# Value heads 1 to 3 as one job of seven half-size products

## The chip, the cores and the metric

The kernel runs on one core of a Trainium2 chip. The metric is the device time of one execution in microseconds, lower is better. The core has five engines with an instruction stream each: TensorE (PE, matmuls, with weight loads in PEld), VectorE (DVE), ScalarE (ACT), GpSimd (POOL) and SyncE (SP), which issues the DMAs. SBUF holds the working tiles, PSUM the matmuls' results, HBM everything that is stored between stages.

## The reference

One layer of a hybrid decoder, T = 1024 tokens, width D = 1024. A normalised input h is projected by one matrix w_in into all that follows. Four heads of gated linear attention (GLA) take a query and key of 128, a value of 256, a rank-16 decay code and a gate each; eight heads of stick-breaking attention take 128 each; two merge gates weigh the branches.

```python
h = rmsnorm(x, norm_g)
qg, kg, vg, gg, r, qs, ks, vs, gs, m = split(h @ w_in)   # vg: 1024 columns = 4 heads of 256
log_a = log_sigmoid(r @ w_dec_up + b_dec) / 16
y_a = (rmsnorm(gla(qg, kg, vg, log_a), gla_g) * silu(gg)) @ w_pa
y_b = (stick_breaking(qs, ks, vs) * silu(gs)) @ w_pb
out = rmsnorm(x + (sigmoid(ma) * y_a + sigmoid(mb) * y_b) @ w_o, final_g)
```

Everything is float32. The change touches vg = h @ w_in[:, value columns], the way in which it is stored, and sums of blocks of h.

## The kernel before

Precision comes from splitting: each float32 operand is written as a high part that TensorE takes in one pass (the copy on ACT rounds it) and a low part, the rest (a subtraction on DVE). A product then is three matmuls, high by high, high by low, low by high. The helper `split` makes the two parts.

**First stage** (pool p0). For each of the eight blocks of 128 tokens: `norm_a` squares and sums x on ACT, `norm_b` scales it on DVE, `turn_x` transposes it on PE into a PSUM tile `tr`, one for each half g of the columns, and splits the result into the quarter blocks `hq[n, g]` (n: first or second 512 tokens). These are named ha11, ha12, ha21, ha22, with h or l for the parts. In the gaps `first_v` computes value head 0 and the decay code, 272 columns, for the block before.

**Value stage.** `v_unit` makes heads 1 to 3 in 24 units (three heads, eight blocks), each 24 matmuls of 256 columns in `proj_n` (L221). Each result is split by ACT and DVE into a staged tile `o` and stored in its two parts in `d_gv` by `store_v`, two blocks a DMA. Beside it POOL puts the blocks together again (`whole`, high + low), and forms the sums S1 to S4 of quarter blocks (`sum2`); ACT and DVE split them (`part`). A list `line` sets which of these stands beside which unit.

**Pairs.** From there every projection is a job of seven products of half size, after Winograd: with the block sums S1 to S4 of h, and sums T1 to T4 of the weights, seven products of 512 x 512 x 512 take the place of eight. The class `Pairs` runs the jobs one after another: the 1 MB load of a job's weights (tile `raw`), the sums of its weights on POOL (`tt`), four splits, seven units. Its first two loads and first three splits are issued when `Pairs` is made. Beside job 0 the decay code is made from the rank-16 result: `wup` is loaded, `wst` and `rst` are split from it and from the turned `rcode`, and a matmul of the two gives the decay's logits. The first unit's product is copied out by ACT (`f`), and the third unit needs that copy done, since it goes on in the same PSUM bank.

**Later.** The GLA stage loads values and gates a block at a time (`gl_load`) and works on it in `gl_local`; then stick-breaking attention and output.

SP issues all DMAs in its program's order. ACT, DVE and PE take their instructions in program order as well; in the value stage of before the order of ACT and DVE is that of the code (`manual_schedule`), elsewhere a planner sets it.

Of the kernel before, what the change touches and what calls it, by code (L numbers as in the profile page):

```python
# [67 lines left out]
class Pairs:  # L68
# [33 lines left out]
def hybrid_layer(ctx: ExitStack, tc: tile.TileContext, x, norm_g, w_in, w_up, b_dec,  # L102
# [20 lines left out]
    def dram_set(nm, count, shape, dt=F32):  # L123
        return [dram.tile(shape, dt, tag=f"{nm}{i}", name=f"d_{nm}{i}") for i in range(count)]
# [220 lines left out]

    vend = const.tile([P, SB_H, NT], F32, tag="vend", name="vend")

    def store_v(key, i, tb):

        if tb % 2:  # L350
            nc.sync.dma_start(d_gv[i][:, tb - 1:tb + 1], vst.pop((key, tb // 2)).bitcast(F32))

    def v_stage(key, tb):
        if tb % 2 == 0:
            vst[key, tb // 2] = (stage().rearrange("p a b -> p (a b)")
                                 .rearrange("p (t s c) -> p t s c", t=2, s=2))
        return vst[key, tb // 2][:, tb % 2]

    with tc.tile_pool(name="p0", bufs=3, reuse_waits="tile") as p0:
        gb = p0.tile([P, D], F32, tag="gb", name="gb", bufs=1)  # L360
# [40 lines left out]
        ws0.append(load_vr(1))  # L401
        for tb in range(2, NT):
            load_x(tb)

        def first_v(tb):
            pt = proj_n(rows_of(ws0), hq, tb, VR, early=tb == 0)
            st = v_stage(0, tb)
            split(pt[:, 0:DV], st[:, 0], st[:, 1])
            store_v(0, 0, tb)
            nc.vector.tensor_copy(rcode[:, tb], pt[:, DV:VR])  # L410

        def turn_x(tb, gs=(0, 1)):
            xs = by_parity(xss[tb])
            for g in gs:
                pt = ps.tile([P, HALF], F32, tag="tr", name="tr")
                for j in range(4):
                    nc.tensor.transpose(pt[:, j * P:(j + 1) * P], xs[:, g, j], ident)
                cs = slice(tb % 4 * P, (tb % 4 + 1) * P)
                q = hq[tb // 4, g]
                split(pt.rearrange("p (a b) -> p a b", a=4), q[0][:, :, cs], q[1][:, :, cs])  # L420

        with tc.manual_schedule(engines={mybir.EngineType.Activation, mybir.EngineType.DVE}):
            norm_a(0)
# [15 lines left out]
            norm_a(1)  # L439
            nc.vector.tensor_sub(lo0, raw0, hi0.bitcast(F32))  # L440
            nc.scalar.activation(hi1, raw1, AF.Copy)
            norm_b(1, 0)
            nc.vector.tensor_sub(lo1, raw1, hi1.bitcast(F32))
            norm_b(1, 1)
            ws0 = [w[1:] for w in ws0]
            for tb in range(1, NT):
                if tb + 1 < NT:
                    norm_a(tb + 1)
                turn_x(tb)
                if tb + 1 < NT:  # L450
                    norm_b(tb + 1)
                first_v(tb - 1)
            first_v(NT - 1)
        load_cols(p0.tile([22, P], F32, tag="vrow", name="vrow", bufs=1))


    v_ctx = ExitStack()
    vw = v_ctx.enter_context(tc.tile_pool(name="vw", bufs=2, reuse_waits="tile"))
    vws, vraw = {}, {}

    def v_load(c0, key):
        vraw[key] = raw_tile()
        nc.sync.dma_start(vraw[key], w_in[:, c0:c0 + DV].rearrange("(k p) c -> p k c", p=P))

    def v_split(key, i):

        hi, lo = ((vw.tile([P, 4, DV], F32R, tag="v" + s, name="v" + s) if i else
                   w_tile(s).rearrange("p k c -> p (k c)").rearrange("p (k c) -> p k c", c=DV)) for s in "hl")
        split(vraw[key][:, 4 * i:4 * i + 4], hi, lo)
        vws.setdefault(key, []).append((hi, lo))  # L470
# [10 lines left out]
    vjobs = [(i, C_GV + i * DV) for i in range(1, GLA_H)]  # L481
    v_load(vjobs[0][1], vjobs[0][0])
    v_load(vjobs[1][1], vjobs[1][0])
    vline = []
    for i, (key, _) in enumerate(vjobs):
        for tb in range(NT):
            vline.append((lambda key=key, tb=tb: v_unit(key, tb), True))
            if tb in (3, 4) and i + 1 < len(vjobs):
                vline.append((lambda key=vjobs[i + 1][0], a=tb - 3: v_split(key, a), False))
            if tb == 5 and i + 2 < len(vjobs):  # L490
                vline.append((lambda job=vjobs[i + 2]: v_load(job[1], job[0]), False))
    st = Line(vline)


    f = {}

    def fresh(nm):
        f[nm] = ev.tile([P, HALF], F32, tag="f", name="f")
        return f[nm]

    def whole(nm, q, j):
        return lambda: nc.gpsimd.tensor_add(fresh(nm), q[0][:, j].bitcast(F32), q[1][:, j].bitcast(F32))

    def sum2(nm, a, b, op=ALU.subtract):
        return lambda: nc.gpsimd.tensor_tensor(fresh(nm), f[a], f[b], op=op)

    def part(nm, j):
        def go():
            if nm not in comb:
                comb[nm] = quarter(a21b, nm, "a21") if nm == "S2" else quarter(sp, nm, nm.lower())  # L510
            split(f[nm], comb[nm][0][:, j], comb[nm][1][:, j])

        return go

    line = [[] for _ in range(25)]
    for j in range(4):
        ops = [whole("a21", hq[1, 0], j), whole("a22", hq[1, 1], j), sum2("S1", "a21", "a22", ALU.add),
               whole("a11", hq[0, 0], j), sum2("S3", "a11", "a21"), sum2("S2", "S1", "a11"),
               whole("a12", hq[0, 1], j), sum2("S4", "a12", "S2")]
        at = [(8 * j + i) * 22 // 32 for i in range(8)]  # L520
        for i, op in enumerate(ops):
            line[at[i]].append(op)
        for i, nm in ((2, "S1"), (4, "S3"), (5, "S2"), (7, "S4")):
            line[at[i] + 2].insert(0, part(nm, j))

    manual = ExitStack()
    manual.enter_context(tc.manual_schedule(engines={mybir.EngineType.Activation, mybir.EngineType.DVE}))
    for a in range(2):
        v_split(vjobs[0][0], a)
    st.run(1)  # L530
    for i, s in enumerate("hl"):
        nc.sync.dma_start(d_a21[i], hq[1, 0][i].bitcast(F32))
    for ops in line:
        for op in ops:
            op()
        st.run(1)
    manual.close()


    def qk_pair(c0, i, dst):  # L540
        def evict(J, n, bank, add):
# [97 lines left out]
    st.run()  # L639
    v_ctx.close()  # L640
    a21_ctx.close()
    late = []
    pairs = Pairs([merge_pair(C_MA, i, d_ga) for i in range(3)] +
                  gla_qk(0) + [gg_pair(0), gg_pair(1)] + gla_qk(1) + [gg_pair(2), gg_pair(3)] +
                  [f for i in range(4) for f in (qk_pair(C_SQ, i, d_q), qk_pair(C_SK, i, d_k))] +
                  [sg_pair(i) for i in range(3)] + [merge_pair(C_MB, i, d_gb) for i in range(4)] +
                  [sv_pair(i) for i in range(4)] + [merge_pair(C_MA, 3, d_ga)], late)

    dq_ctx = ExitStack()
    dq = dq_ctx.enter_context(tc.tile_pool(name="dq", bufs=1, reuse_waits="tile"))  # L650
# [844 lines left out]
```

## Time and profile before

| | us |
|---|---|
| median of 3 runs | 1190.33 (1189.4 to 1190.63) |
| profiled execution, span | 1187.3 |
| profiled execution, own device time | not recorded, only its span |
| PE busy | 1174.5 |
| DVE busy | 834.8 |
| ACT busy | 535.3 |
| POOL busy | 294.4 |

Times are from the start of the span. "Busy" is when an engine executes; what a row waits for stands in square brackets behind it, as the idle time before it and the instruction that ended it. Matmuls overlap in PE's pipeline, so that a row's duration is longer than the distance to the next start; the distance between starts is what a matmul costs in a row of many. For a DMA the row of SP is only its issue; the landing is given in a line of its own as the smallest, middle and largest time from issue to landing.

### The profile page before, as it was taken

How to read it: one execution, taken by the hardware profiler on the slowest of the kernel's cores; microseconds unless marked ns; L12 is line 12 of the kernel's file. 1: busy time of each engine (PE TensorE's matmuls, PEld its weight loads, DVE VectorE, ACT ScalarE, POOL GpSimd, SP SyncE). 2: the span in 40 equal slices, each digit the busy share in tenths (PEclk: the TensorE clock that was granted, in tenths of full speed). 3: DMA queues.
4: the chain of work that ended last, by engine and by line, in shares of the span. 5: the costliest groups of instructions: out<-in, count | busy, mean ns of one | idle time of the engine just before them, and what ended most of it. 6: DMA issues, size and time to landing. Idle time of an engine off the chain costs nothing.

```text
span 1187.3 us, 17020 instructions
## 1 busy us (share of the span) xinstructions
PE 1174.5 (99%) x6051; PEld 989.3 (83%) x6051; DVE 834.8 (70%) x1388; ACT 535.3 (45%) x1000; POOL 294.4 (25%) x249
## 2 busy tenths in 40 slices
PE   8999999999999999999999999999999999999997
PEld 8999878888888888888888887888888888888886
DVE  6475876787677777767656567547787876488986
ACT  5343763333444444444434444334444544275543
POOL 1496513143333233224223223000000000700001
PEclk9999999999999999999999999999999999999999
DMA  7434349998356566655454447899766556848652
GB/s 286 196 133 153 129 164 317 331 316 275 120 187 222 183 213 215 188 187 169 145 168 149 133 138 229 254 322 320 258 218 224 186 168 192 288 160 285 220 195 106
DMA packets 189377, 247.65 MB, mean 209 GB/s; under 512 B 12358, under 2 KB 121948, under 8 KB 187756
## 3 DMA queue, kind: packets, MB, share of 16 engines
q1 hardware_dynamic: 188716, 245.52, 61.6%
q8 instruction: 47, 0.77, 0.3%
q10 hardware_dynamic: 576, 1.05, 0.2%
q14 instruction: 38, 0.31, 0.1%
HBM read 154.25 MB, written 92.27 MB: 208 GB/s over the span
## 4 chain that ended last, share of the span: by engine, by line
PE 89%; DVE 4%; ACT 2%; DMA 2%; issue 1%; SPq 0%; POOL 0%; ACTq 0%; DVEq 0%
PE pp L268 15%; PE pp L269 15%; PE pp L270 15%; PE pp L221 8%; PE pp L204 3%; PE pp L203 3%; PE pp L202 3%; PE tr L990 1%; PE av L1013 1%; PE av L1012 1%; PE av L1011 1%; PE z L972 1%; PE z L974 1%; PE z L973 1%; PE xb L1379 1%
## 5 line engine op out<-in xcount | busy, mean ns | idle before, releaser
L164 DVE TENSOR_TENSOR wl<-tt,wh 128x1024 fp32r<-128x1024 f32 x62 | 77.5, 1250 | 53.2 <-ACT wh L163 52.9
L307 DVE TENSOR_TENSOR f<-pp,f 128x512 f32<-128x512 f32 x93 | 64.0, 688 | 72.1 <-PE pp L270 68.2
L242 POOL TENSOR_TENSOR tt<-raw 128x512 f32<-128x512 f32 x31 | 44.6, 1438 | 225.2 <-DVE wl L164 204.8
L163 ACT ACTIVATE wh<-tt 128x1024 fp32r<-128x1024 f32 x62 | 65.6, 1058 | 74.7 <-PE pp L269 68.8
L274 ACT ACTIVATE f<-pp 128x512 f32<-128x512 f32 x93 | 55.1, 593 | 88.2 <-PE pp L270 84.9
L978 DVE TENSOR_TENSOR_SCAN be<-be,m 128x128 f32<-128x128 f32 (+3 forms) x64 | 86.1, 1347 | 4.5 <-ACT be L975 4.3
L163 ACT ACTIVATE wh<-raw 128x1024 fp32r<-128x1024 f32 x44 | 46.5, 1059 | 84.0 <-PE pp L269 48.1
L164 DVE TENSOR_TENSOR wl<-raw,wh 128x1024 fp32r<-128x1024 f32 x44 | 64.3, 1463 | 18.7 <-ACT wh L163 18.1
L229 POOL TENSOR_TENSOR r<-r,nhalf 128x1 f32<-128x1 f32 x40 | 24.4, 609 | 198.3 <-DVE r L228 177.2
L1162 POOL TENSOR_TENSOR N<-A,A 128x512 f32<-128x512 f32 x4 | 6.6, 1658 | 244.0 <-PE pp L204 244.0
L975 ACT ACTIVATE be<-z 128x384 f32<-128x384 f32 (+4 forms) x96 | 47.1, 495 | 19.7 <-PE z L974 17.3
L268 PE MATMUL pp<-ha11h,wh 128*128 128x512 f32 x124 | 49.2, 397 | 0.0
L268 PE MATMUL pp<-S2h,wh 128*128 128x512 f32 x124 | 49.1, 396 | 0.0
L268 PE MATMUL pp<-S1h,wh 128*128 128x512 f32 x124 | 49.1, 396 | 0.0
L268 PE MATMUL pp<-ha12h,wh 128*128 128x512 f32 x124 | 49.0, 395 | 0.0
L268 PE MATMUL pp<-ha22h,wh 128*128 128x512 f32 x124 | 48.9, 394 | 0.2 <-DVE f L307 0.2
L268 PE MATMUL pp<-S3h,wh 128*128 128x512 f32 x124 | 48.8, 394 | 0.0
L268 PE MATMUL pp<-S4h,dh 128*128 128x512 f32 x124 | 48.6, 392 | 0.0
L270 PE MATMUL pp<-S1h,wl 128*128 128x512 f32 x124 | 48.4, 390 | 0.0
L270 PE MATMUL pp<-ha11h,wl 128*128 128x512 f32 x124 | 48.4, 390 | 0.0
L269 PE MATMUL pp<-S2l,wh 128*128 128x512 f32 x124 | 48.3, 390 | 0.0
L270 PE MATMUL pp<-ha12h,wl 128*128 128x512 f32 x124 | 48.3, 390 | 0.0
(519 smaller groups left out, 3844.4 us busy)
## 6 DMA issues: line engine op xcount, KB each, us to landing
raw<-in_w_in_dram SPq DMA_DIRECT2D x34, 1024.0 KB, 6.0
d_gv<-o SPq DMA_DIRECT2D x16, 512.0 KB, 2.6
d_t<-t SPq DMA_DIRECT2D x16, 512.0 KB, 6.4
v<-d_gv SPq DMA_DIRECT2D x32, 256.0 KB, 3.0
d_ogl<-o SPq DMA_DIRECT2D x64, 128.0 KB, 2.6
d_q<-o SPq DMA_DIRECT2D x16, 512.0 KB, 3.8
d_k<-o SPq DMA_DIRECT2D x16, 512.0 KB, 3.5
d_v<-o SPq DMA_DIRECT2D x32, 256.0 KB, 2.5
```

The costliest lines, as they stand in the source:

```text
L163: nc.scalar.activation(hi, src, AF.Copy)
L164: eng.tensor_sub(lo, src, hi.bitcast(F32))
L202: nc.tensor.matmul(pt, whi[:, kb], h_, start=kb == 0, stop=False)
L221: nc.tensor.matmul(pt[:, 0:n], *ops[kb][i], start=k == 0, stop=k == 3 * KB - 1)
L242: nc.gpsimd.tensor_sub(t1, b[:, 0, 1], b[:, 0, 0])
L268: nc.tensor.matmul(pt, bh[:, j], ah[:, j], start=first and j == 0, stop=False, skip_group_check=True)
L269: nc.tensor.matmul(pt, bh[:, j], al[:, j], start=False, stop=False, skip_group_check=True)
L270: nc.tensor.matmul(pt, bl[:, j], ah[:, j], start=False, stop=j == 3, skip_group_check=True)
L274: nc.scalar.activation(t[nm], t[bank], AF.Copy)
L307: nc.vector.tensor_add(add, bank, add)
L975: nc.scalar.activation(om[:, off + pc * w:off + (pc + 1) * w], zt[:, 0:w], AF.Sigmoid, scale=-inv_sqrt)
L978: nc.vector.tensor_tensor_scan(rest, rest, m1[:, off:T][:, ::-1], 1.0, op0=ALU.mult, op1=ALU.max)
```

## The change

The values of heads 1 to 3, 768 columns, become one job of the same seven-product form: halves of 512 tokens by halves of 512 rows by halves of 384 columns. There are 56 items (`v_item`): seven products, two row halves `jp`, four token blocks t, each six matmuls of 384 columns. That makes 336 matmuls instead of 576 of 256 columns.

- **Whole blocks** of h are no longer rebuilt from their parts by POOL. ACT copies each turned block from PSUM in the first stage (`whole`), 16 copies of 128x512.
- **Sums of h** S1 to S4 are made on DVE (`h_sum`), 16 of 128x512, and split (`h_split`); the sums of the value weights T1 to T4 too (`vq_sum`, four of 128x1536). The weights are split in 14 parts of 768 columns (`vq_split`), three of these inside the first stage at blocks 4, 5 and 6.
- **Results** are added up by ACT and DVE (`v_evict`) in tiles s1, s5, p7 and c and stored unsplit by 40 small DMAs (`v_put`, 64 or 128 KB). c has two tiles, "dh" and "dl". `d_gv` holds one value instead of two parts; `gl_local` splits each loaded block (one more split of 128x256 for each of 32 blocks). Head 0's result is copied once instead of split.
- **The order** of PE, ACT and DVE in the job is written out: the table `due` gives the items after which the sums, splits and evictions stand. The two first loads and three first splits of the pair jobs (`pairs.first`) stand at items 40, 46, 49, 53 and 55.
- The x tiles and first weights move to other slots of the same memory; the weight half B22 is loaded after the first stage.

The core of the diff:

```diff
-        for j in self.jobs[:2]:
-            j["load"]()
-        for s in range(3):
-            self.jobs[0]["split"][s]()
+        self.first = [j["load"] for j in self.jobs[:2]] + self.jobs[0]["split"][:3]
...
-    d_gv = dram_set("gv", GLA_H, [P, NT, 2, DV])
+    d_gv = dram_set("gv", GLA_H, [P, NT, DV])
...
+    VPRODUCTS = [("A11", "B11"), ("A12", "B21"), ("A22", "T4"), ("S1", "T1"), ("S2", "T2"), ("S4", "B22"), ("S3", "T3")]
+    def vq_split(u, jp):
+        src = vq[VPRODUCTS[u][1]][:, 2 * jp:2 * jp + 2]
...
+        split(src, hi, lo)
+    def vq_sum(nm):
...
+        nc.vector.tensor_sub(dst, vq[x1], vq[x2_])
+    VW_AT = {4: (0, 0), 5: (0, 1), 6: (1, 0)}
+    def whole(tb, g, pt):
...
+        nc.scalar.activation(wh[n, g, t], pt, AF.Copy)
...
         def first_v(tb):
             pt = proj_n(rows_of(ws0), hq, tb, VR, early=tb == 0)
-            st = v_stage(0, tb)
-            split(pt[:, 0:DV], st[:, 0], st[:, 1])
-            store_v(0, 0, tb)
+            st = v_stage(tb)
+            nc.vector.tensor_copy(st[:, tb % 2], pt[:, 0:DV])
+            if tb % 2:
+                nc.sync.dma_start(d_gv[0][:, tb - 1:tb + 1], st)
...
                 split(pt.rearrange("p (a b) -> p a b", a=4), q[0][:, :, cs], q[1][:, :, cs])
+                whole(tb, g, pt.rearrange("p (a b) -> p a b", a=4))
...
-    def v_unit(i, tb):
-        st = v_stage(i, tb)
-        split(proj_n(rows_of(vws[i]), hq, tb), st[:, 0], st[:, 1])
-        store_v(i, i, tb)
...
-        return lambda: nc.gpsimd.tensor_add(fresh(nm), q[0][:, j].bitcast(F32), q[1][:, j].bitcast(F32))
...
-        return lambda: nc.gpsimd.tensor_tensor(fresh(nm), f[a], f[b], op=op)
...
+    vq_load("B22")
     for i, s in enumerate("hl"):
         nc.sync.dma_start(d_a21[i], hq[1, 0][i].bitcast(F32))
...
+    def v_put(n, J, t, c):
+        tb = 4 * n + t
+        for h, c0, o0, w in (((1, 0, 0, DV), (2, 0, DV, P)) if J == 0 else ((2, P, 0, P), (3, 0, P, DV))):
+            nc.sync.dma_start(d_gv[h][:, tb, c0:c0 + w], c[:, o0:o0 + w])
...
+    def v_item(u, jp, t, bank):
+        (ah, al), (bh, bl) = comb[VPRODUCTS[u][0]], vsp[u, jp]
+        ts = slice(t * P, (t + 1) * P)
+        for i in range(2):
+            j = 2 * jp + i
+            nc.tensor.matmul(bank, ah[:, j, ts], bh[:, i], start=u < 4 and j == 0, stop=False, skip_group_check=True)
...
+        elif u == 5:
+            c = sw.tile([P, 4, P], F32, tag="d" + "hl"[t % 2], name="c", bufs=1).rearrange("p a c -> p (a c)")[:, 0:VH]
+            nc.scalar.activation(c, vy[t], AF.Copy)
+            nc.vector.tensor_add(c, vx[t], c)
+            v_put(0, 1, t, c)
...
+    for u in range(7):
+        if u != 4:
+            for t in range(4):
+                due[8 * u + 5 + t].insert(0, (v_evict, (u, t)))
+    for k, fn in zip((40, 46, 49, 53, 55), pairs.first):
+        at(k, fn)
...
+        t["v"] = split2(t["vr"], [P, DV], "v")
```

In the first stage, ACT between two norms, before (blocks 4 and 5; `o` is head 0's result):

```order
L387 ACTIVATE xs,ssq<-xt 128x1024
L163 ACTIVATE ha21h<-tr 128x4x128
L163 ACTIVATE ha22h<-tr 128x4x128
L163 ACTIVATE o<-pp 128x256
L387 ACTIVATE xs,ssq<-xt 128x1024
```

and now (w, f, o here are the whole blocks):

```order
L433 ACTIVATE xs,ssq<-xt 128x1024
L160 ACTIVATE ha21h<-tr 128x4x128
L403 ACTIVATE w<-tr 128x512
L160 ACTIVATE ha22h<-tr 128x4x128
L403 ACTIVATE o<-tr 128x512
L160 ACTIVATE wh<-vq 128x768
L433 ACTIVATE xs,ssq<-xt 128x1024
```

Each whole copy stands ahead of the next high half, and waits on DVE's low half of the same tile. DVE at block 6, now:

```order
L456 COPY vst<-pp 128x256
L459 COPY rcode<-pp 128x16
L161 TENSOR_TENSOR wl<-vq,wh 128x768
L225 TENSOR_SCALAR r<-ssq 128x1
L381 TENSOR_TENSOR vq<-raw,vq 128x1536
L161 TENSOR_TENSOR ha21l<-tr,ha21h 128x4x128
L161 TENSOR_TENSOR ha22l<-tr,ha22h 128x4x128
```

The sum T1 (128x1536) and a weight split stand ahead of the block's low halves; before, only the small row of `r` stood there. SP in the sixth product, now (c_1144, c_1159 and so on are the tiles c of blocks t = 0, 1, 2, 3; the first and third share a buffer, and the second and fourth):

```order
L655 DMA d_gv2_134<-c_1144 128x128
L655 DMA d_gv3_135<-c_1144 128x256
L235 DMA raw_1164<-in_w_in_dram 128x8x256
L655 DMA d_gv2_134<-c_1159 128x128
L655 DMA d_gv3_135<-c_1159 128x256
L655 DMA d_gv2_134<-c_1177 128x128
L655 DMA d_gv3_135<-c_1177 128x256
```

The 1 MB load of the second pair job stands between the stores of t = 0 and those of t = 1. SP where the value stage ends, before:

```order
L238 DMA raw<-in_w_in_dram 128x8x256
L351 DMA d_gv_134<-o 128x1024
L238 DMA raw<-in_w_in_dram 128x8x256
L351 DMA d_gv_134<-o 128x1024
L351 DMA d_gv_135<-o 128x1024 x3
L655 DMA wup<-in_w_dec_up_dram 16x512
L351 DMA d_gv_135<-o 128x1024
L582 DMA d_ga_142<-f 128x512
```

and now:

```order
L655 DMA d_gv_134<-s_995 128x128
L655 DMA d_gv_135<-s_995 128x256
L655 DMA d_gv_133<-p_912 128x256
L655 DMA d_gv_134<-p_912 128x128
L235 DMA raw<-in_w_in_dram 128x8x256
L744 DMA wup<-in_w_dec_up_dram 16x512
L564 DMA d_ga_142<-f 128x512
```

The load of wup stood ahead of the last value store; it now stands behind all of them and behind the load of the third pair job.

More of the change, by code (lines that the diff above doesn't have):

```diff
@@ new lines, in hybrid_layer, with four @@
+    VW_AT = {4: (0, 0), 5: (0, 1), 6: (1, 0)}
+    wh = {}
+    def four(i, nm):
+        return slot(i, [P, 4 * HALF], nm).rearrange("p (t j c) -> p t j c", t=4, c=P)
+    def whole(tb, g, pt):
+        n, t = divmod(tb, 4)
+        if (n, g) == (0, 1):
+            wh[n, g, t] = ev.tile([P, HALF], F32, tag="f", name="f").rearrange("p (j c) -> p j c", c=P)
+        elif (n, g) == (1, 1):
+            if t % 2 == 0:
+                two = stage().bitcast(F32)
+                for i in range(2):
+                    wh[n, g, t + i] = two[:, i].rearrange("p (j c) -> p j c", c=P)
+        elif t == 0:
+            w = four((3, 5)[n], "w")
+            for i in range(4):
+                wh[n, g, i] = w[:, i]
+        nc.scalar.activation(wh[n, g, t], pt, AF.Copy)
@@ L441, in hybrid_layer @@
             nc.scalar.activation(hi1, raw1, AF.Copy)
+            for g in range(2):
+                whole(0, g, pts[g])
             norm_b(1, 0)
@@ L457, in hybrid_layer @@
     v_ctx = ExitStack()
[L458 to L470, printed above, removed]
-    def v_unit(i, tb):
-        st = v_stage(i, tb)
-        split(proj_n(rows_of(vws[i]), hq, tb), st[:, 0], st[:, 1])
-        store_v(i, i, tb)
+    vw = v_ctx.enter_context(tc.tile_pool(name="vw", bufs=1, reuse_waits="tile"))
     def ch3(a):
@@ L480, in hybrid_layer @@
     ebl = const.tile([P, GLA_H, NCH], F32, tag="ebl", name="ebl")
[L481 to L501, printed above, removed]
-        return lambda: nc.gpsimd.tensor_add(fresh(nm), q[0][:, j].bitcast(F32), q[1][:, j].bitcast(F32))
-    def sum2(nm, a, b, op=ALU.subtract):
-        return lambda: nc.gpsimd.tensor_tensor(fresh(nm), f[a], f[b], op=op)
[L507 to L530, printed above, removed]
+    vq_load("B22")
     for i, s in enumerate("hl"):
         nc.sync.dma_start(d_a21[i], hq[1, 0][i].bitcast(F32))
[L533 to L537, printed above, removed]
     def qk_pair(c0, i, dst):
@@ L647, in hybrid_layer, with h_sum @@
                   [sv_pair(i) for i in range(4)] + [merge_pair(C_MA, 3, d_ga)], late)
+    s1 = slot(6, [P, 4 * HALF], "s1").rearrange("p (t c) -> p t c", t=4)
+    DEST = {"S1": (2, 4), "S2": (0, 1), "S4": (6, 7), "S3": (3, 5)}
+    def h_sum(nm, t):
+        a11, a12, a21, a22 = (wh[n, g, t] for n, g in ((0, 0), (0, 1), (1, 0), (1, 1)))
+        if nm == "S1":
+            nc.vector.tensor_add(a22, a21, a22)
+        elif nm == "S2":
+            nc.vector.tensor_sub(a22, a22, a11)
+        elif nm == "S4":
+            nc.vector.tensor_sub(a12, a12, a22)
+        else:
+            wh["S3", t] = ev.tile([P, HALF], F32, tag="f", name="f").rearrange("p (j c) -> p j c", c=P)
+            nc.vector.tensor_sub(wh["S3", t], a11, a21)
@@ new lines, in h_split @@
+    def h_split(nm, t):
+        if nm not in comb:
+            comb[nm] = tuple((a21b if i < 2 else sp).tile([P, 4, HALF], F32R, tag=SLOTS[i], name=nm, bufs=1)
+                             for i in DEST[nm])
+        src = {"S1": lambda: wh[1, 1, t], "S2": lambda: wh[1, 1, t], "S3": lambda: wh["S3", t],
+               "S4": lambda: wh[0, 1, t]}[nm]()
+        split(src, *(a[:, :, t * P:(t + 1) * P] for a in comb[nm]))
+    def v_put(n, J, t, c):
+        tb = 4 * n + t
+        for h, c0, o0, w in (((1, 0, 0, DV), (2, 0, DV, P)) if J == 0 else ((2, P, 0, P), (3, 0, P, DV))):
+            nc.sync.dma_start(d_gv[h][:, tb, c0:c0 + w], c[:, o0:o0 + w])
@@ new lines, in hybrid_layer, with v_bank @@
+    vx = [ps.tile([P, HALF], F32, tag=tag, name="vx")[:, 0:VH] for tag in ("z", "z", "tr", "tr")]
+    vy, keep4 = {}, {}
+    def v_bank(u, t):
+        if u in (0, 4, 6):
+            return vx[t]
+        if u != 5:
+            vy[t] = (ps.tile([P, HALF], F32, tag="av", name="vy", bufs=1) if t == 3 else
+                     ps.tile([P, HALF], F32, tag="pp", name="pp", bufs=3))[:, 0:VH]
+        return vy[t]
+    def v_item(u, jp, t, bank):
+        (ah, al), (bh, bl) = comb[VPRODUCTS[u][0]], vsp[u, jp]
+        ts = slice(t * P, (t + 1) * P)
+        for i in range(2):
+            j = 2 * jp + i
+            nc.tensor.matmul(bank, ah[:, j, ts], bh[:, i], start=u < 4 and j == 0, stop=False, skip_group_check=True)
+            nc.tensor.matmul(bank, ah[:, j, ts], bl[:, i], start=False, stop=False, skip_group_check=True)
+            nc.tensor.matmul(bank, al[:, j, ts], bh[:, i], start=False, stop=j == 3, skip_group_check=True)
@@ new lines, in hybrid_layer @@
+    for u in range(7):
+        if u != 4:
+            for t in range(4):
+                due[8 * u + 5 + t].insert(0, (v_evict, (u, t)))
+    for k, fn in zip((40, 46, 49, 53, 55), pairs.first):
+        at(k, fn)
+    manual = ExitStack()
+    manual.enter_context(tc.manual_schedule(engines={mybir.EngineType.Activation, mybir.EngineType.DVE,
+                                                     mybir.EngineType.PE}))
+    for k in range(60):
+        if k < 56:
+            u, r = divmod(k, 8)
+            jp, t = divmod(r, 4)
+            if jp == 0:
+                bank = v_bank(u, t)
+            else:
+                bank = vx[t] if u in (0, 4, 6) else vy[t]
+            v_item(u, jp, t, bank)
+        for fn, args in due[k]:
+            fn(*args)
```

79 lines of the change are left out of this document (64 added, 15 removed).

## The prediction

> **What bounds the kernel now.** I read the page first, then windows by stage, then the timeline around the three places where the change works. The page says that TensorE (PE) is the bound.
>
> ```profile
> span 1187.3 us, 17020 instructions
> PE 1174.5 (99%) x6051; PEld 989.3 (83%) x6051; DVE 834.8 (70%) x1388; ACT 535.3 (45%) x1000; POOL 294.4 (25%) x249
> PE 89%; DVE 4%; ACT 2%; DMA 2%; issue 1%; SPq 0%; POOL 0%; ACTq 0%; DVEq 0%
> ```
>
> PE is idle for only 1187.3 − 1174.5 = 12.8 us of the profiled execution. Removing matmuls therefore pays in full, and each wait that the change puts on PE is paid in full too. The windows, whose columns are PE, weight loads, DVE, ACT and POOL busy (instructions), show where the slack is; the last line is the second window again with only L221, the matmuls of the value stage.
>
> ```profile
> 0.00:44.60 44.60, 40.94 (x292) 38.29 (x292) 28.12 (x52) 23.55 (x43) 9.70 (x18) 1.00 0.67 248
> 44.60:113.80 69.20, 69.20 (x578) 69.19 (x578) 39.86 (x49) 24.19 (x47) 51.25 (x34) 1.00 0.45 161
> 113.80:120.40 6.60, 6.60 (x35) 5.35 (x33) 3.48 (x5) 5.42 (x10) 2.44 (x4) 1.00 0.21 84
> 120.40:700.00 579.60, 579.25 (x2775) 475.91 (x2774) 411.17 (x746) 262.26 (x490) 189.21 (x154) 1.00 0.61 200
> 44.60:113.80 69.20, 69.20 (x576) 69.15 (x576) 1.00 0.45 161
> ```
>
> **Part 1, the products.** The value stage is 576 matmuls 256 wide in 69.20 us, 0.120 us each. Now there are 336, 384 wide. That width, and 512, stand in later stages:
>
> ```profile
> 776.29 0.39 PE L202 MATMUL pp<-ha11h,wh 128*128 128x512 f32 x1
> 776.51 0.39 PE L203 MATMUL pp<-ha11l,wh 128*128 128x512 f32 x1
> ...
> 788.47 0.34 PE L973 MATMUL z<-k,q 128*128 128x384 f32 x1
> 788.64 0.34 PE L974 MATMUL z<-k,q 128*128 128x384 f32 x1
> ```
>
> The starts at 384 are 0.17 apart, and halfway between 0.120 and the 0.22 to 0.23 at 512 lies 0.174; I take 0.173. 336 × 0.173 = 58.2 us, so **−11.0 us**. This is also the most the change can bring: 1179.3.
>
> **Part 2, the whole blocks in the first stage.** One turned block goes through this chain now:
>
> ```profile
> 22.57 0.30 PE L417 MATMUL tr<-ident,xs 128*128 128x128 f32 x1
> 27.13 1.03 PE L417 MATMUL tr<-ident,xs 128*128 128x128 f32 x8
> 27.77 0.60 ACT L163 ACTIVATE ha21h<-tr 128x512 fp32r<-128x512 f32 x1 [1.42 <-PE tr L417]
> 28.26 0.59 ACT L163 ACTIVATE ha22h<-tr 128x512 fp32r<-128x512 f32 x1
> 28.40 0.69 DVE L164 TENSOR_TENSOR ha21l<-tr,ha21h 128x512 fp32r<-128x512 f32 x1 [1.02 <-ACT ha21h L163]
> 29.00 0.68 DVE L164 TENSOR_TENSOR ha22l<-tr,ha22h 128x512 fp32r<-128x512 f32 x1
> 29.60 1.28 DVE L397 SCALAR_TENSOR_TENSOR xs<-xt,r,gb 128x1024 f32<-128x1024 f32 x1
> 31.02 0.52 PE L417 MATMUL tr<-ident,xs 128*128 128x128 f32 x3
> 38.87 0.30 PE L417 MATMUL tr<-ident,xs 128*128 128x128 f32 x1
> 44.57 0.38 PE L221 MATMUL pp<-wh,ha11h 128*128 128x256 f32 x1
> ```
>
> From one turn to the next it is 31.02 − 27.13 = 3.89 us: 0.64 to the high half, 0.63 to the low half on DVE, 0.60 for the second low half, 0.60, then 1.42 for the norm and the next turn. The two high halves follow each other on ACT at 0.49. In the changed order ACT runs high 0, whole 0, high 1, whole 1, and each whole copy waits for DVE's low half of the same block to end, so that the two don't read one PSUM tile together. High 1 then stands behind whole 0, which stands behind low 0: 0.64 + 0.63 + 0.72 (low 0's latency, rounded from its 0.69) + 0.49 + 0.63 + 0.60 + 1.42 = 5.13 us, 1.24 more per block. Nothing covers it: PE has only the 3.89 us of work per block that it has now, and no value product can run before its half of h is complete. Two things come on top. ACT's high part of a 768-wide weight split stands ahead of block 6's turn (0.3 us), and DVE's first sum T1, 128x1536, stands ahead of block 6's low half (about 1.6 us beyond its slack, estimated at 1.77 from the 1024 and 512 wide rows below). The turn of block 3 comes 1.5 us later than the 22.57 above, and the four cycles from there to block 7's turn take 5.13 + 5.13 + 5.45 + 6.73 = 22.4 instead of 38.87 − 22.57 = 16.3. Block 7's tail (turn to the end of the first head's matmuls) takes 6.3 instead of 44.57 − 38.87 = 5.7. That is 1.5 + 6.1 + 0.6 = 8.2 us later; 16 of the new matmuls, 2.8 us, get in before. **+5.4 us.** Bounds: 0 if whole copy and low half overlap, +8.2 if nothing fills.
>
> What the trace shows of two readers is ACT's ha22h at 28.26 beside DVE's ha21l at 28.40, so reading from PSUM in parallel is possible, but these are two tiles. The Trainium skill, PSUM — Partial Sum Buffer, section "PSUM bank collisions raise a hardware error", says that two engines which read one bank at once collide, reads against reads included, and that software must keep them apart. By the row alone this term would be near 0 and the sum near 1187.4; by the page the 5.4 us stand, as summed. No run here shows which.
>
> **Part 3, the value job's vector work.** DVE gets sums and low halves: 11 splits 768 wide (0.96), 16 block sums and 16 block splits 512 wide (0.69), three sums 1536 wide (1.77), 16 evictions 384 wide (0.55); 10.6 + 11.0 + 11.0 + 5.3 + 8.8 = 46.7 us within about 56, interpolated between the rows of the next fence. ACT has about 27, from its high parts and copies at the durations of its rows. Both stay under PE, hidden as long as the due items leave a few us. POOL loses its 51.25 us of block sums, on which nobody then waits. Price 0, bounds 0 to +4.
>
> **Part 4, the last third: stores behind loads.** Everything goes through SP's queue in order. What a small transfer costs behind a 1 MB weight load:
>
> ```profile
> 62.08 0.38 SPq L238 DMA_DIRECT2D raw<-in_w_in_dram  x1
> DMA to landing us min/median/max: 6.0/6.0/6.0
> 63.02 0.32 SPq L351 DMA_DIRECT2D d_gv<-o  x1
> DMA to landing us min/median/max: 7.8/7.8/7.8
> d_gv<-o SPq DMA_DIRECT2D x16, 512.0 KB, 2.6
> 136.17 0.50 SPq L582 DMA_DIRECT2D d_ga<-f  x1
> DMA to landing us min/median/max: 5.2/5.2/5.2
> ```
>
> The load issued at 62.08 lands at 68.1, and the store issued 0.9 later lands at 70.85, 7.8 us after its issue instead of 2.6. A store waits out the load ahead of it. In the changed kernel the sixth product's results go out from two alternating buffers (tiles c). The first pair jobs' loads stand among these stores: the second buffer's stores are issued just behind a 1 MB load, and the fourth result, which needs that buffer back, waits for them. Item 44 ends at 0; the split that frees the load's tile ends near 2.4, the load is issued there, its stores at 3.0 to 3.4, landing at about 8.5 to 9.5; the fourth copy and its sum need 1.0 more; PE wants that bank at item 51, six items of 6 × 0.173 = 1.04 us after 0, at 6.2. **+3.6 us** (2.9 to 4.4; 0 if stores aren't held).
>
> **Part 5, the handover to the pair jobs.** Rows at the boundary:
>
> ```profile
> 113.79 0.60 PE L677 MATMUL tr<-ident,rcode 128*16 128x128 f32 x4
> 113.98 0.33 SPq L655 DMA_DIRECT2D wup<-in_w_dec_up_dram  x1
> 113.99 0.38 ACT L163 ACTIVATE o<-pp 128x256 fp32r<-128x256 f32 x1 [2.49 <-PE pp L221]
> 114.41 0.42 DVE L164 TENSOR_TENSOR o<-pp,o 128x256 fp32r<-128x256 f32 x1 [2.45 <-ACT o L163]
> 115.80 1.28 ACT L668 ACTIVATE wst<-wup 16x512 fp32r<-16x512 f32 x2 [0.91 <-DMA wup<-in_w_dec_up_dram]
> 117.10 1.19 ACT L668 ACTIVATE rst<-tr 16x512 fp32r<-16x512 f32 x2
> 118.31 1.06 ACT L163 ACTIVATE wh<-tt 128x1024 fp32r<-128x1024 f32 x1
> 119.28 0.58 ACT L274 ACTIVATE f<-pp 128x512 f32<-128x512 f32 x1
> 119.40 1.22 DVE L164 TENSOR_TENSOR wl<-tt,wh 128x1024 fp32r<-128x1024 f32 x1 [0.35 <-ACT wh L163]
> 120.18 0.39 PE L684 MATMUL tr<-rst,wst 128*128 128x512 f32 x1
> ```
>
> Here wup is issued 0.2 us after the value stage ends and lands 1.8 us later. ACT then does wst, rst, wh and the copy f one after the other, 119.86 − 115.80 = 4.06 us, and PE, with 6.4 us of work between, isn't held. In the changed order wup stands behind the last 4 value stores, which follow DVE's last additions about 2.8 us after the stage's end X (0.5 to start, a split of 0.69, three additions of 0.55), and behind another 1 MB load. By the 6.0 above it lands at X + 8.9 to 9.5. The same ACT chain ends at X + 13.0 to 13.6. PE reaches the product that needs f, with one product more ahead of it (36 matmuls 512 wide at 0.228, 8.2 us, and the two turns of rcode, 0.7 together), at X + 8.9. **+4.5 us** (4.1 to 4.7; 0.5 if wup isn't held by the load).
>
> The Trainium skill, DMA: Bandwidth & Descriptors, section "Queues, rings and completion order", states that each DMA engine takes descriptors in ring order but that completion is not first in, first out per issuing engine. Read as overtaking, parts 4 and 5 would fall to about 0.5 and the time to 1185; the trace, with 7.8 us for a store behind a load, doesn't bear that out.
>
> **Part 6, the rest.** 32 more splits of 256 columns on ACT (0.38) and DVE (0.42) in the attention stage: 12 and 13 us within 579.60, where PE is busy 579.25, DVE 411.17, ACT 262.26. Price 0, up to +2 where they sit ahead of a scan. Half the bytes per value store and load, hidden before: 0.
>
> **Sum:** −11.0 + 5.4 + 3.6 + 4.5 = +2.5 us, on the profiled execution, of which only the span of 1187.3 is given, it is a span of 1189.8; the median of the runs is 3.0 above that span, the launch's part, which nothing here touches, so 1190.33 + 2.5 = **1192.8 us**.
>
> **Rivals.** (a) *Small stores overtake loads* (or the waited-for tiles are free earlier): parts 4 and 5 are about 0.5, time 1185.2. For it speaks that 64 and 128 KB transfers are smaller than any in the rows above; against it d_ga, 256 KB, 5.2 us behind a load issued half a microsecond before. If only one of the two waits goes, 1188.8 to 1189.2. (b) *All gain*: copies hide too, near 1180; the fixed order speaks against it. (c) *Slower, by DVE in the value job*: it is at 46.7 of 56 us, and each item's sums stand ahead of the split on which the next product waits. It decides as soon as DVE runs late by more than the 3 to 4 items by which the splits are due early; the second sum T2 needs a load behind the 1 MB stores of h at the end of stage one, with only about 1.8 us in hand. Price +3 to +6, time 1196 to 1199. (d) *PE's clock or pitch differ*: 384 columns at 0.180 would add 2.4 us; the windows show the granted clock at 1.00.
>
> **How the numbers follow.** No change that can be told is within 0.2%, 2.4 us: 1187.9 to 1192.7. All as summed 0.42 (1190 to 1196 by the bounds of parts 2, 4 and 5); only one of the two queue waits 0.19; neither 0.15; the whole copies hidden and both queue waits there, 1187.4, 0.05; all gain 0.05; DVE or T2 late besides 0.14. The first case splits about evenly at 1192.7, tilted to slower: slower 0.41, same 0.29, faster 0.30. The range leaves out the all-gain case and the edges: 1184.5 to 1199.
>
> **What would show it.** 336 matmuls 384 wide at a pitch of 0.173. Turns 5.1 us apart in the first stage, with ACT's whole copy starting when DVE's low half ends. The first stage ending near 53, and the value job, with 320 of its matmuls left at 0.173, ending near X = 108 plus part 4's wait. A gap on PE of 3 to 4 us in the seventh product, released by an addition that waited for a c copy, and that by a DMA. A gap of 4 to 5 us about 9 us into the pair jobs, released by ACT's f; wup's landing 6 us after its issue. I am wrong if turns stay 3.9 apart, if those gaps are absent, or if DVE, not a DMA, releases PE within the value job.

## The result and the profile after

The changed kernel takes 1203.76 us (1203.64 to 1205.42, 4 runs) against 1190.01 for the kernel before in the same comparison: ratio 1.0112, interval 1.0098 to 1.0127. It is slower, on the side forecast, but by 13.7 us instead of 2.5, and outside the range. The head of the page:

```profile
span 1202.1 us, 16630 instructions
PE 1170.7 (97%) x5811; PEld 981.5 (82%) x5811; DVE 863.1 (72%) x1440; ACT 553.0 (46%) x1040; POOL 248.6 (21%) x217
PE 85%; DVE 6%; DMA 4%; ACT 3%; issue 2%; SPq 0%; POOL 0%; ACTq 0%; DVEq 0%; POOLq 0%
```

PE's idle time went from 12.8 to 1202.1 − 1170.7 = 31.4 us. Its busy time fell by only 3.8, in part because some of it is at a lower clock. The waits of PE, longest first, with the total, the number of times and the longest:

```profile
PE vx L673 <- DVE c L691: 5.8, 1, 5.8
PE tr L773 <- DVE rst L759: 5.7, 1, 5.7
```

The first is the wait that part 4 named, at its place and with its chain. The second lies where part 5 put it, 9.3 us behind the value job's end, but PE stands at another instruction there: at the matmul of rst and wst, released by DVE's low part of rst, not at the product that needs ACT's f. Windows of the steady value job, of the stretch behind the first wait and of that behind the second (the column behind the counts is the granted clock):

```profile
53.30:103.70 50.40, 50.40 (x292) 50.20 (x290) 42.74 (x55) 23.44 (x42) 7.24 (x5) 1.00 0.28 88
105.00:115.00 10.00, 5.38 (x22) 5.38 (x23) 3.19 (x5) 3.01 (x4) 0.00 (x0) 0.66 0.21 67
125.00:135.00 10.00, 4.29 (x11) 2.62 (x10) 4.19 (x6) 6.08 (x9) 2.25 (x4) 0.76 0.26 91
```

In the first window PE never waits; 290 matmuls in 50.40 us are 0.174 each. In the other two the clock is 0.66 and 0.76, where the windows of the kernel before show 1.00 up to 700 us. The turns of the first stage on PE's timeline:

```profile
18.93 1.04 PE L466 MATMUL tr<-ident,xs 128*128 128x128 f32 x8
24.15 1.04 PE L466 MATMUL tr<-ident,xs 128*128 128x128 f32 x8
...
39.96 1.05 PE L466 MATMUL tr<-ident,xs 128*128 128x128 f32 x8
46.75 1.04 PE L466 MATMUL tr<-ident,xs 128*128 128x128 f32 x8
```

They come 5.2 us apart, 5.4 and 6.8 before the last two; before it was 3.9, with the last at 38.87. The first wait on the timeline of SP, ACT, DVE and PE, and the times from issue to landing of the load (issued at 99.86) and of the first store behind it (100.34):

```profile
99.86 0.38 SPq L235 DMA_DIRECT2D raw<-in_w_in_dram  x1
103.48 0.34 PE L675 MATMUL vx<-wh,S 128*128 128x384 f32 x1
108.49 0.49 ACT L690 ACTIVATE c<-vy 128x384 f32<-128x384 f32 x1 [6.80 <-DMA d_gv<-c]
109.01 0.56 DVE L691 TENSOR_TENSOR c<-vx,c 128x384 f32<-128x384 f32 x1 [6.73 <-ACT c L690]
109.62 0.69 PE L673 MATMUL vx<-wh,S 128*128 128x384 f32 x1 [5.80 <-DVE c L691]
110.11 0.52 PE L674 MATMUL vx<-wl,S 128*128 128x384 f32 x1
110.43 0.52 PE L675 MATMUL vx<-wh,S 128*128 128x384 f32 x1
113.39 0.33 PE L673 MATMUL vx<-wh,S 128*128 128x384 f32 x1
```

```profile
DMA to landing us min/median/max: 8.0/8.0/8.0
...
DMA to landing us min/median/max: 7.7/7.7/7.7
```

The chain reads upwards: PE waits for DVE's addition, this for ACT's copy, this for a store, and the store lands 0.2 us behind the load. Behind the wait the matmuls start 0.32 apart (110.11, 110.43) until about 113, then 0.17. The handover:

```profile
116.51 0.39 PE L265 MATMUL pp<-ha11h,wh 128*128 128x512 f32 x1
122.73 0.41 SPq L235 DMA_DIRECT2D raw<-in_w_in_dram  x1
123.19 0.57 SPq L744 DMA_DIRECT2D wup<-in_w_dec_up_dram  x1
128.23 1.28 ACT L757 ACTIVATE wst<-wup 16x512 fp32r<-16x512 f32 x2 [14.62 <-DMA wup<-in_w_dec_up_dram]
131.53 0.80 PE L773 MATMUL tr<-rst,wst 128*128 128x512 f32 x1 [5.71 <-DVE rst L759]
131.69 0.58 ACT L271 ACTIVATE f<-pp 128x512 f32<-128x512 f32 x1
132.91 0.63 PE L266 MATMUL pp<-S,wh 128*128 128x512 f32 x1
133.34 0.63 PE L267 MATMUL pp<-S,wl 128*128 128x512 f32 x1
```

The value job ends at 116.5; wup is issued only 6.7 us later, lands about 5 us after that, and ACT waits for it 14.6 us. Here too the matmuls behind run slow, 0.43 apart. To see what has been lost by the middle of the kernel, I use one group, the turns of the attention stage on PE, by its first and last start. Before and after:

```profile
L874 PE MATMUL tr<-ident,on x64: 270/272/327, 330.0 to 726.4; 128*128 128x128 f32 x64
```

```profile
L964 PE MATMUL tr<-ident,on x64: 270/272/328, 342.8 to 739.2; 128*128 128x128 f32 x64
```

By 330 us the kernel is 12.8 behind, and it stays at 12.8 to 726. The span is longer by 14.8; the other 2.0 come later, in stick-breaking attention. The medians differ by only 13.7: in the runs on record whose time and span are both known the time is mostly 1.7 to 2.0 us longer than the span, so that the profiled execution of the kernel before, with its span of 1187.3, was itself about 1 us quicker than the median.

### The profile page after: what moved, and what is told of

Its sections match the earlier page's. It is cut to its first block, busy times and chain, and to the rows that moved or that the text cites. A ratio compares the mean times of both kernels' runs of the same rounds, so it can differ in the third digit from the quotient of the medians.

```text
span 1202.1 us, 16630 instructions
## 1 busy us (share of the span) xinstructions
PE 1170.7 (97%) x5811; PEld 981.5 (82%) x5811; DVE 863.1 (72%) x1440; ACT 553.0 (46%) x1040; POOL 248.6 (21%) x217
## 4 chain that ended last, share of the span: by engine, by line
PE 85%; DVE 6%; DMA 4%; ACT 3%; issue 2%; SPq 0%; POOL 0%; ACTq 0%; DVEq 0%; POOLq 0%
PE pp L265 16%; PE pp L266 15%; PE pp L267 15%; PE pp L199 3%; PE pp L201 3%; PE pp L200 3%; PE av L1103 1%; PE av L1102 1%; PE av L1101 1%; PE tr L1080 1%; PE z L1062 1%; PE xb L1469 1%; PE xb L1468 1%; PE xb L1467 1%; PE z L1064 1%
## 5 line engine op out<-in xcount | busy, mean ns | idle before, releaser
L265 PE MATMUL pp<-S,wh 128*128 128x512 f32 x372 | 148.0, 398 | 0.0
L267 PE MATMUL pp<-S,wl 128*128 128x512 f32 x372 | 145.7, 392 | 0.0
L266 PE MATMUL pp<-S,wh 128*128 128x512 f32 x372 | 145.7, 392 | 0.0
L160 ACT ACTIVATE wh<-raw 128x1024 fp32r<-128x1024 f32 (+1 forms) x47 | 48.4, 1030 | 82.8 <-PE pp L266 49.8
L265 PEld LDWEIGHTS pp<-S,wh 128*128 128x128 f32 x372 | 71.1, 191 | 15.0 <-ACT f L271 0.7
L267 PEld LDWEIGHTS pp<-S,wl 128*128 128x128 f32 x372 | 70.3, 189 | 15.0
L266 PEld LDWEIGHTS pp<-S,wh 128*128 128x128 f32 x372 | 70.4, 189 | 13.8
L161 DVE TENSOR_TENSOR wl<-raw,wh 128x1024 fp32r<-128x1024 f32 (+1 forms) x47 | 65.5, 1394 | 18.2 <-ACT wh L160 17.5
L265 PE MATMUL pp<-S,dh 128*128 128x512 f32 x124 | 48.7, 393 | 0.6 <-ACT f L271 0.6
L242 POOL TENSOR_TENSOR tt<-raw,tt 128x512 f32<-128x512 f32 x31 | 48.3, 1557 | 2.3
```

The costliest lines, as they stand in the source:

```text
L160: nc.scalar.activation(hi, src, AF.Copy)
L161: eng.tensor_sub(lo, src, hi.bitcast(F32))
L242: nc.gpsimd.tensor_sub(t4, b[:, 1, 0], t2)
L265: nc.tensor.matmul(pt, bh[:, j], ah[:, j], start=first and j == 0, stop=False, skip_group_check=True)
L266: nc.tensor.matmul(pt, bh[:, j], al[:, j], start=False, stop=False, skip_group_check=True)
L267: nc.tensor.matmul(pt, bl[:, j], ah[:, j], start=False, stop=j == 3, skip_group_check=True)
```

## The experiments

**Own buffers for the results c** (e1_c_four).

```diff
+            if t < 2:
                 c = sw.tile([P, 4, P], F32, tag="d" + "hl"[t % 2], name="c", bufs=1)...
+            else:
+                if t == 2:
+                    keep4["c"] = stage().bitcast(F32)
+                c = keep4["c"][:, t - 2, 0:VH]
```

> The results of the sixth product for blocks 2 and 3 go to two buffers of their own (halves of a tile that is free by then), so that no copy waits for a store. All loads and stores stay where they are. Theory (the store behind the 1 MB load holds the buffer, and the granted clock falls after the wait): PE's gap of 5.8 us in the seventh product is gone, and so are the 1.7 us that its 30 matmuls took longer than 0.174 each; the value job ends 7.5 us earlier and the time is about 1196.3. The handover's wait may shift by 1 to 2 us either way, since the stores then queue closer to the load. Rival (DVE is late there, and the DMA only seems to be the releaser): the gap stays within 2 us of 5.8 and the time at 1202 to 1204.

1196.24 us, 1.0048 (1.0033 to 1.0063) of before: 7.5 less than the changed kernel. The wait for c is gone, and the middle of the kernel moves by 342.8 − 335.4 = 7.4:

```profile
L969 PE MATMUL tr<-ident,on x64: 270/272/328, 335.4 to 731.9; 128*128 128x128 f32 x64
```

The wait at the handover stays, 5.9. So the first wait with its slow matmuls costs 7.4 us, as the theory had it.

**wup early** (e2_wup_first).

```diff
+    wup = stage().bitcast(F32)[0:RANK, 0]
+    def wup_load():
+        nc.sync.dma_start(wup, w_up)
+    at(30, wup_load)
...
-    wup = dq.tile([RANK, GLA_H * P], F32, tag="wup", name="wup")
-    nc.sync.dma_start(wup, w_up)
```

> Only the 16x512 load of wup is issued early, into a tile that is free then, ahead of the value job's stores; the clearing of rst also no longer waits for the last stores' memory. Theory (wup behind the load and the last stores holds ACT, f and the pair jobs' third product): the gap of 5.7 us on PE, the 2.9 us by which the matmuls behind it run slow, and two waits of 1.0 us together are gone: about 1194.2. Rival (PE would wait there anyway, for the weights' splits or for DVE's additions): a gap of 3 us or more stays and the time is 1199 or above.

The edit also lets POOL clear the tile of rst at 94.6 instead of 123.4 us, where the clearing waited for a store; the two belong together here. 1196.99 us, 1.0054 (1.0039 to 1.0069). The middle of the kernel moves by 8.1, less than the 9.6 expected, and PE's waits show why:

```profile
PE vx L673 <- DVE c L691: 4.5, 1, 4.5
PE pp L265 <- ACT f L271: 1.6, 2, 1.1
```

```profile
L968 PE MATMUL tr<-ident,on x64: 270/272/328, 334.7 to 731.1; 128*128 128x128 f32 x64
```

The gap of 5.7 is gone; waits for f remain, 1.6 together. And 1.3 of the 8.1 is a shorter first wait, 4.5 for 5.8: the second pair job's load took 6.7 us in this execution instead of 8.0, which nothing shows to be the edit's doing. The theory holds, the remainder was priced too high.

**Both** (e3_c_wup).

> Both edits, own buffers for c and the early load of wup. Theory: the two waits are independent and add: 1203.8 - 7.5 - 9.6 = 1186.7, faster than the kernel before by 3 to 4 us, with the products' 11 us less the first stage's loss left. Rival (the waits are one thing, the stores' queue, and come back at the next load): 1190 to 1196.

1188.14 us, 0.9979 (0.9969 to 0.9988): faster than before by 0.2%. The middle of the kernel stands at 327.7, 15.1 before that of the changed kernel; the two single edits gave 7.4 + 8.1 = 15.5. They add nearly in full. Beside own buffers for c, where no wait for c blurs it, the early wup is worth 335.4 − 327.7 = 7.7.

**Whole copies behind both high halves** (e4_whole_after).

```diff
                 split(pt.rearrange("p (a b) -> p a b", a=4), q[0][:, :, cs], q[1][:, :, cs])
-                whole(tb, g, pt.rearrange("p (a b) -> p a b", a=4))
+                turned[g] = pt.rearrange("p (a b) -> p a b", a=4)
+            for g in gs:
+                whole(tb, g, turned[g])
```

> In the first stage both whole copies stand behind both high halves on ACT, otherwise as in the changed kernel. Theory (each whole copy waits for DVE's low half of its tile and holds back the next high half): the turns of blocks 3 to 6 come 3.9 us apart again instead of 5.2, 5 us are won up to block 6, the delay by the sum T1 stays: about 1198.7. Rival (PE's own work or the loads set the pace there): turns stay above 4.8 us apart, and the time is 1202 to 1204.

1199.02 us, 1.0069 (1.0052 to 1.0085), 4.7 less than the changed kernel; the middle moves by 4.6. PE's turns are 3.9 apart:

```profile
20.10 1.04 PE L467 MATMUL tr<-ident,xs 128*128 128x128 f32 x8
24.00 1.06 PE L467 MATMUL tr<-ident,xs 128*128 128x128 f32 x8
27.93 1.06 PE L467 MATMUL tr<-ident,xs 128*128 128x128 f32 x8
```

The first copy still waits for DVE's low half, 0.27 us; the copies only no longer stand ahead of the other half. The order on ACT was the cost, not the copies. The 4.6 in the middle is not a clean price: the last turn comes 5.0 us earlier (41.75 for 46.75), but PE then waits 1.0 us for a split of a block sum, and the two long waits are 4.4 and 5.2 instead of 5.8 and 5.7.

**The sum T1 later** (e10_t1_late).

```diff
             first_v(NT - 1)
+            vq_sum("T1")
...
-    for k, nm in ((0, "T1"), (1, "T2"), (6, "T4"), (17, "T3")):
+    for k, nm in ((1, "T2"), (6, "T4"), (17, "T3")):
```

> The changed kernel with one thing moved: DVE's sum T1 stands behind the last first-head result of the first stage instead of ahead of block 6's low half. Theory: the turn of block 7 comes 1.6 us earlier (near 45.2), the value job begins 1.6 us earlier and the whole kernel ends 1.6 us earlier, near 1202.1. Rival (the sum fits into DVE's slack there, or comes back as a later T2): no change, 1203.8.

The turn of block 7 comes at 45.60 instead of 46.75, and the middle of the kernel moves by 342.8 − 341.1 = 1.7, near the 1.6 expected. The time doesn't show it: 1204.31 us, 1.0099 (1.0081 to 1.0117), with single runs from 1199.4 to 1204.64. In the profiled one, the slowest of them, PE waits late in the kernel:

```profile
PE av L1102 <- ACT afh L160: 2.5, 1, 2.5
...
856.00:858.00 2.00, 2.00 (x7) 1.82 (x8) 2.00 (x5) 1.31 (x5) 0.00 (x0) 0.50 0.50 151
```

The second line is the window behind this wait: the granted clock is 0.50 here as well. So this run alone says little on the whole time. It is the stretch to the middle that shows T1's cost; the late stage is taken up below.

**All four edits** (e6_all).

> Own buffers for c, early wup, both whole copies behind both high halves, and the sum T1 behind the last first-head result of the first stage instead of ahead of block 6's low half. Theory (the terms add): 1188.1 of the two queue edits less 4.7 for the whole copies (what the edit alone brought) less 1.5 for T1: about 1182. Rival (the time won in the first stage comes back as a wait of the value job on its weights B22 and T2, which do not load earlier): 1185 to 1187.

1180.82 us, 0.9928 (0.9916 to 0.994): faster than both kernels, by 9 us than before. The middle stands at 321.5, 21.3 before the changed kernel's; the four single edits gave 7.4 + 8.1 + 4.6 + 1.7 = 21.8.

```profile
L977 PE MATMUL tr<-ident,on x64: 270/272/332, 321.5 to 718.0; 128*128 128x128 f32 x64
```

**Matmuls in the wait** (e7_warm).

```diff
+            if k == 51:
+                idle = ps.tile([P, HALF], F32, tag="pp", name="idle", bufs=3)[:, 0:VH]
+                for n in range(24):
+                    nc.tensor.matmul(idle, comb["S3"][0][:, 0, 0:P], vsp[6, 0][0][:, 0], start=True, stop=True)
             v_item(u, jp, t, bank)
```

> The changed kernel with 24 more matmuls of 384 columns ahead of item 51, into a bank that nobody reads; they take 4.2 us, inside the wait of 4.4 to 5.8 us for c. No wait is taken away. Theory (the idle time itself lowers the granted clock, and the matmuls behind it then run slow): the 30 matmuls behind the wait run at 0.174 each, the granted clock between 105 and 115 us stays near 1.00, and the time falls by 1 to 1.7 us, to about 1202.3, although the kernel does more work. Rival (the matmuls behind the wait are slow for another reason, such as DMA traffic to the same memory): no gain, 1203.8 or above.

1200.16 us, 1.0088 (1.0075 to 1.0101). With 24 matmuls more, the window behind the wait shows the full clock:

```profile
105.00:115.00 10.00, 8.42 (x49) 8.10 (x48) 4.73 (x7) 3.02 (x4) 0.00 (x0) 1.00 0.31 103
```

```profile
L968 PE MATMUL tr<-ident,on x64: 270/272/328, 341.2 to 737.7; 128*128 128x128 f32 x64
```

The middle moves by 1.6, the part that the clock takes of the first wait's 7.4. The remaining 2 us of the gain in time lie in the late stage. The Trainium skill, TensorE: Matmul & The Clock Gate, section "What's actually happening", states that a monitor halves the array's clock after an idle window of about 3.4 us and gives it back after as long a busy one. The trace agrees here: 0.32 against 0.174 per matmul, from 109.6 to about 113.0, 3.4 us. Across the runs the slow stretch behind a long wait lasts from about 3.1 us (e10) to 5.7 (e1, at the handover). A wait of 1.6 us (this run) has no slow matmuls behind it, but the one of 2.5 late in e10 has, so that less idle time than 3.4 us was enough there.

**Stores of c from ACT's queue** (e8_act_queue).

```diff
-            v_put(0, 1, t, c)
+            v_put(0, 1, t, c, nc.scalar)
```

> Only the eight stores of the c tiles are issued by ACT on its own queue instead of by SP behind the load. Theory (a store waits for the load ahead of it in the same queue): they land in 2 to 3 us, the gap in the seventh product is gone or under 1 us, time about 1196.5. Rival (the load fills the 16 DMA engines whichever queue a store comes from): the stores land only 5 us or more after their issue, the gap stays above 3 us, time 1200 or above.

1203.39 us, 1.0115 (1.0102 to 1.0128), no gain, as the rival had it. PE's wait for c, the load, the two stores of the second tile c, and the load and the first of these stores from issue to landing:

```profile
PE vx L673 <- DVE c L691: 5.0, 3, 4.0
...
102.94 0.38 SPq L235 DMA_DIRECT2D raw<-in_w_in_dram  x1
103.42 0.81 ACTq L655 DMA_DIRECT2D d_gv<-c  x2
...
DMA to landing us min/median/max: 6.9/6.9/6.9
...
DMA to landing us min/median/max: 5.6/5.6/5.6
```

The store now lands 0.8 us ahead of the load instead of 0.2 behind it, but its 5.6 us are far from the 1.7 of the first tile's store, which had no load ahead of it. So it isn't SP's queue alone that holds it; a transfer of 1 MB in flight is enough for a good part of it. Why 64 KB on another queue doesn't get an equal share, this doesn't tell. The whole time is no fair price of the other queue: ACT issues these stores in its own order, each behind DVE's addition, and its next weight split behind them, so that load and store leave 3.1 us later than in the changed kernel (99.86 and 100.34).

**The load behind the stores** (e9_load_late).

```diff
-    for k, fn in zip((40, 46, 49, 53, 55), pairs.first):
+    for k, fn in zip((14, 50, 49, 53, 55), pairs.first):
...
-                                                     mybir.EngineType.PE}))
+                                                     mybir.EngineType.PE, mybir.EngineType.SP}))
```

> The changed kernel with its two c buffers as they are; only the second pair job's 1 MB load is moved behind the last store of a c tile (SP's order in the value job is fixed for that, the first job's load stays early). Theory (the load ahead of or beside the store is what holds it, not the number of buffers): the c stores land in about 2 us, the gap of 5.8 us and the slow matmuls behind it are gone, 7.3 us. The last stores then stand behind the load, and the handover's gap stays at 5 to 6 us. About 1196.4. Rival (two buffers are too few even at 2 us a store, or the wait moves to the handover in full): 1199 or above.

SP now follows the code's order too; the first pair job's load stands at item 14, near where the planner had issued it (66 us). 1198.58 us, 1.0061 (1.0047 to 1.0075), 5.2 less than the changed kernel, between what the theory and the rival had forecast. PE's waits at the two places, and the landing of the second tile's two stores, on which the fourth result waits:

```profile
PE tr L773 <- DVE rst L759: 5.7, 1, 5.7
PE vx L673 <- DVE c L691: 1.4, 1, 1.4
...
DMA to landing us min/median/max: 3.3/3.3/3.4
```

With the load out of the way these stores take 3.3 to 3.4 us instead of 7.5 to 7.7, and the wait for c falls from 5.8 to 1.4, with the same two buffers. It isn't gone, because they land later than the 2 us expected; those of the first tile took 1.7 and 2.0, of the third 2.0. Why the second tile's took longer with no load beside them stays open; at 2.0 the wait of 1.4 would be gone, by an estimate from these figures. Fixing SP's order also made the last turn of the first stage 1.0 us later (47.77 for 46.75), about the rest of the missing gain.

**Unsplit values alone** (b1_unsplit), on the kernel before:

```diff
-    d_gv = dram_set("gv", GLA_H, [P, NT, 2, DV])
+    d_gv = dram_set("gv", GLA_H, [P, NT, DV])
...
-            split(pt[:, 0:DV], st[:, 0], st[:, 1])
+            nc.scalar.activation(st, pt[:, 0:DV], AF.Copy)
...
+        t["v"] = split2(t["vr"], [P, DV], "v")
```

> The kernel before with one part of the change alone: values stored unsplit (one copy by ACT instead of a split) and split again when the attention stage loads them. Theory (32 more splits on ACT and DVE are hidden under PE, half the bytes were hidden too): within 0.15% of before, 1190.3, with no shift of PE through the attention stage. Rival (these splits or the changed loads are what delays the stick-breaking stage by 0.9 to 2.2 us in all versions of the changed kernel so far): 1191.3 to 1192.5, with the shift appearing behind 835 us.

1190.46 us, 1.0003 (0.999 to 1.0016): no difference. The attention stage runs where it ran before:

```profile
L874 PE MATMUL tr<-ident,on x64: 269/272/328, 330.0 to 726.4; 128*128 128x128 f32 x64
```

## Why the prediction was wrong, and where it was right

| step | forecast | measured |
|---|---|---|
| Part 1, products | −11.0 | −10.8 (69.20 − 336 × 50.40 / 290) |
| Part 2, first stage | +5.4 | +6.2 (e3 to e6) |
| Part 3, DVE in the value job | 0 | 0 (no wait in 50.40 us, DVE 42.74) |
| Part 4, stores of c | +3.6 | +7.4 (e1: 5.8 wait, 1.6 clock) |
| Part 5, handover | +4.5 | +7.7 (e1 to e3), and 1.6 of waits for f that stay |
| Part 6, splits in attention | 0 | 0 (396.4 us from first to last turn in both) |
| late stage | 0 | +2.0 in the profiled executions, not settled |

The kernel with all four edits stands 8.5 below before in the middle where −10.8 was to be had. Of these 2.3 us 1.6 are still waits for f at the handover; 0.7 are not placed. With them the column gives the shift in the middle: −10.8 + 6.2 + 7.4 + 7.7 + 2.3 = 12.8.

The sum put the losses in the right stages and failed by two mis-sized terms, parts 4 and 5. Their waits were too short, and the slow matmuls behind them were put at nothing.

- **The clock after a wait** was left out of both. The prediction looked at PE's clock only as rival (d), and took the windows' 1.00 as a sign that it would stay; but these windows hold no wait of more than 1.4 us of PE, so they could not show it. In part 4 it costs 1.6 us, by e7. In part 5 the matmuls start 0.43 apart instead of 0.23 for some 5 us; what that costs there was not measured apart from the wait. By these figures it would be some 2.5 us, an estimate.
- **Part 4's wait** was 5.8, not 3.6. Counted from item 44's end (97.4), the load was issued at 2.4 and PE stood at the wait at 6.2 to 6.4, as worked out. But the load landed 8.0 us after its issue, where I took the 6.0 of one row; the store behind it landed at 10.6 instead of 8.5 to 9.5, and the copy and the sum were done 1.6 later instead of 1.0. (The prediction's own times give 3.3 to 4.3 for this term, not 2.9 to 4.4.) The trace held a range, of which the row was the middle; all 31 loads of the pair jobs in the kernel before, from issue to landing:

```profile
DMA to landing us min/median/max: 4.7/5.9/8.9
```

  The size is in part chance: in e2 and e4, whose code is the same here, the load took 6.7 and 6.6 us and the wait was 4.5 and 4.4, still above 3.6.
- **Part 5's wait** was 5.7, at rst instead of f. wup was issued 6.7 us after the value job's end; I had put the last store near 3. DVE's last addition ended 2.6 us after it, as worked out, but the last 16 small stores leave SP at about 0.4 us each, so that the row of them, not this addition, decides. (The trace has 32 of these stores in all, not the 40 named above.) The load cost less than feared (5.2 instead of 6.0).
- **The order in SP's queue**, on which parts 4 and 5 rest, is only part of the mechanism. In the eight traces in which SP issues the load and then this store, the load takes 6.6 to 8.1 us and the store lands 0.2 to 0.3 us behind it each time, as the prediction had it. But e8 takes the order away, and the store still takes 5.6 us, against 3.4 without the load (e9), so that a load in flight holds it on another queue too. The Trainium skill, DMA: Bandwidth & Descriptors, section "Queues, rings and completion order", states that completion isn't first in, first out per issuing engine. No run here shows that: on SP's queue the order was kept, and in e8 the store that landed first had another issuing engine.
- **Part 2** was right within 0.1 us in each cycle (5.13, 5.13, 5.45, 6.73 as worked out; 5.2, 5.2, 5.4, 6.8 measured). The Trainium skill, PSUM — Partial Sum Buffer, section "PSUM bank collisions raise a hardware error", states that two engines that read one bank at once collide. No run here shows that: in each the program keeps the copy and the split apart, and the copies run after the splits. e4 shows that this need not cost anything.
- **The launch.** The prediction put the 3.0 us between the profiled span and the median down to the launch. By the runs on record it is mostly 1.7 to 2.0; the rest is that the profiled execution was a quick one. It changes nothing in the difference that was forecast.

**The late stage.** Behind 739 us the changed kernel loses another 2.0 us. PE's waits there explain 1.2 of it: 0.7 for a gate's load (0.2 before) and 0.7 for ACT's afh. e10 lost 4.5 there, 2.5 of it in one wait with slow matmuls behind it, e6 and e7 nothing, b1 0.6, the other versions of the changed kernel 0.9 to 2.3, though all run the same work there. Each figure is one execution, held against one of the kernel before that was about 1 us quick, and the kernel before ranges from 1189.3 to 1193.09 within one comparison. What causes these losses, and whether the change makes them more likely, stays open.

## What to carry to other kernels

On an engine that is busy 99% of the time, price each new wait twice: its length, and, when it is long (2.5 us and more here, not 1.6), the slow matmuls behind it. When results leave through few small buffers, look at what large transfer is in flight between a buffer's store and its next use, and take its duration as the range that the trace shows; here issuing the stores on ACT's queue didn't help, a buffer more or a load at another moment did. Two instructions in the order of an engine (a copy ahead of the next half, a sum ahead of the block that everyone waits for) took away more than half of what the removed matmuls brought, and moving them gave it back.

## What was not expected of the hardware

A wait of 5.8 us on PE nearly halved the speed of the next 3.4 us of matmuls (0.32 against 0.174 us at 384 columns); late in e10 a wait of 2.5 us was enough for the granted clock to fall to 0.50. Work that nobody needs, put into the first wait (e7), made the kernel faster. A 64 KB store issued by ACT took 5.6 us beside a 1 MB load that SP had issued, where the first tile's store, with no load ahead of it, took 1.7.
